# Larger chunks, three homes and waits on the matmuls in a LoRA forward kernel: what 64-row chunks do to a kernel that lives on its DMA queue

## The chip, the cores and the metric

The kernel runs on one core of one Trainium2 chip. The metric is device time in microseconds (us) of one execution; the tables give medians over repeated executions. A verdict of "faster" or "slower" needs a difference of 2% that the whole 95% interval supports; an interval that reaches across 2% is "unclear". With one core a run is called slow when it is over 1.5% above the fastest run of the same kernel; only fast runs are compared here, and one run that stands alone (state unknown) is marked as such.

## The reference

```python
# x: 16 x 2048 x 256 fp32, W: 256 x 256, lora_A: 256 x 16, lora_B: 16 x 256, lora_E: 16
x_flat = x.reshape(-1, in_dim)              # 32768 rows of 256
y = x_flat @ W
lora_out = ((x_flat @ lora_A) * lora_E) @ lora_B
y = y + scale * lora_out
```

The kernel folds the low-rank path into the weight once (W + A·diag(E)·scale·B), so each row of x is read once, multiplied by one 256 x 256 matrix and written once: 33.6 MB in and 33.6 MB out.

## The kernel before

A *chunk* is 32 rows for each of the 128 partitions (4 MB). A *home* is an SBUF tile that holds a chunk; x is loaded into it, and the result is written over x and stored from it. There are eight chunks and six homes, so chunks 6 and 7 reuse the homes of chunks 0 and 1 and must wait for their stores. All large transfers go through one queue, in this order (L is a load, S a store, then chunk, first row, end row):

```python
ROWS = 32; N_CHUNKS = 8; N_HOMES = 6
ORDER = [
    ("L", 0, 0, 8), ("W",), ("L", 0, 8, 16), ("L", 0, 16, 32),
    ("L", 1, 0, 32), ("L", 2, 0, 32), ("L", 3, 0, 32), ("L", 4, 0, 32), ("L", 5, 0, 32),
    ("S", 0, 0, 32), ("S", 1, 0, 24), ("S", 1, 24, 32),
    ("L", 6, 0, 32), ("L", 7, 0, 32),
    ("S", 2, 0, 32), ("S", 3, 0, 32), ("S", 4, 0, 32), ("S", 5, 0, 32), ("S", 6, 0, 32), ("S", 7, 0, 32),
]
HELD = (5, 0)                      # POOL waits here ...
HOLDERS = (("S", 1, 0, 24),)       # ... until this store has landed
```

Compute goes by *groups* of four rows per partition (64 groups): POOL casts x to bf16, PE transposes it, DVE copies the transposed words out of PSUM, PE multiplies, ACT copies the result from PSUM back into the home. PE takes one semaphore for each hand-over with a wait of its own:

```python
def take(s):
    tensor.wait_ge(s, 1).then_inc(s, -1)

def turn(i):
    take(s_stage)
    words = stage[i % NS][:].bitcast(FP32)
    for b in range(CG):
        ins = tensor.transpose(psum_xt[i % NT][:, b, :], words[:, b, :], ident[:])
    ins.then_inc(s_turned, 1)

def multiply(i):
    take(s_xt); take(s_free)
    for b in range(CG):
        for t in range(KT):
            ins = tensor.matmul(psum_y[i % NY][:, b, :], xt[i % NX][:, b, t::KT], weff[:, t, :], ...)
    ins.then_inc(s_y, 1)
# [...] set-up of the folded weight, the other engines' programs, the launch: cut
```

Of the kernel before, what the change touches and what calls it, by code (L numbers as in the profile page):

```python
# [9 lines left out]
BF16 = mybir.dt.bfloat16  # L10
ALU = mybir.AluOpType


ROWS = 32
N_CHUNKS = 8
N_HOMES = 6

ORDER = [
    ("L", 0, 0, 8),
    ("W",),  # L20
    ("L", 0, 8, 16),
    ("L", 0, 16, 32),
    ("L", 1, 0, 32),
    ("L", 2, 0, 32),
    ("L", 3, 0, 32),
    ("L", 4, 0, 32),
    ("L", 5, 0, 32),
    ("S", 0, 0, 32),
    ("S", 1, 0, 24),
    ("S", 1, 24, 32),  # L30
    ("L", 6, 0, 32),
    ("L", 7, 0, 32),
    ("S", 2, 0, 32),
    ("S", 3, 0, 32),
    ("S", 4, 0, 32),
    ("S", 5, 0, 32),
    ("S", 6, 0, 32),
    ("S", 7, 0, 32),
]

HELD = (5, 0)
HOLDERS = (("S", 1, 0, 24),)

WARM_UP = 2

CG = 4
GPC = ROWS // CG
N_GROUPS = N_CHUNKS * GPC

NS, NX, NT, NY = 2, 2, 2, 2  # L50

UNROLL = 4
# [3 lines left out]
def kernel(  # L56
# [16 lines left out]
    KT = K // P  # L73
    assert N == N_CHUNKS * ROWS * P and K == M and KT == 2

    x_chunks = x_flat.rearrange("(c p b) k -> c p b k", p=P, b=ROWS)
    y_chunks = out_flat.rearrange("(c p b) m -> c p b m", p=P, b=ROWS)

    sbuf, psum, sem = nc.alloc_sbuf_tensor, nc.alloc_psum_tensor, tc.alloc_semaphore
    homes = [sbuf(f"home{h}", [P, ROWS, K], FP32) for h in range(N_HOMES)]  # L80
    stage = [sbuf(f"stage{i}", [P, CG, K], BF16) for i in range(NS)]
    xt = [sbuf(f"xt{i}", [P, CG, P * KT], BF16) for i in range(NX)]
    ident = sbuf("ident", [P, P], FP32)

    w_sb = sbuf("w_sb", [P, KT, M], FP32)
# [4 lines left out]
    weff = sbuf("weff", [P, KT, M], BF16)  # L90
    psum_xt = [psum(f"psum_xt{i}", [P, CG, P], FP32) for i in range(NT)]
    psum_y = [psum(f"psum_y{i}", [P, CG, M], FP32) for i in range(NY)]
# [5 lines left out]
        for op in ORDER  # L98
        if op[0] == "S" and (op in HOLDERS or op[1] < N_CHUNKS - N_HOMES)
    }  # L100
    stored = {op: sem(f"stored_{op[1]}_{op[2]}") for op in ORDER if op in waited}
    stored_rest = nc.alloc_semaphore("stored_rest")
    n_rest = sum(op[0] == "S" and op not in waited for op in ORDER)
    ends = sorted((c * ROWS + e) // CG - 1 for kind, c, s, e in (op for op in ORDER if op[0] == "S"))
    s_ident = sem("ident_made")
    s_pe_set_up = sem("pe_set_up")
    s_ate = sem("ate_made")
    s_stage = sem("staged")
    s_turned = sem("turned")
    s_xt = sem("xt_made")  # L110
    s_y = sem("multiplied")
    s_free = sem("y_free")
    s_done = sem("rows_done")

    def home(c):
        return homes[c % N_HOMES]

    sync, gpsimd, scalar, vector, tensor = nc.sync, nc.gpsimd, nc.scalar, nc.vector, nc.tensor
# [20 lines left out]
    def sync_program():  # L139
        for n, op in enumerate(ORDER):  # L140
# [6 lines left out]
            if kind == "L":  # L147
                for st in stored:
                    if st[1] == c - N_HOMES and st[2] < e and s < st[3]:
                        sync.wait_ge(stored[st], 16)  # L150
# [7 lines left out]
    def gpsimd_program():  # L158
        gpsimd.memset(ident[:], 0.0).then_inc(s_ident, 1)  # L159
        gpsimd.wait_ge(s_ident, 1)  # L160
        gpsimd.affine_select(  # L161
            out=ident[:],
            in_=ident[:],
            compare_op=ALU.not_equal,
            fill=1.0,
            base=0,
            pattern=[[-1, P]],
            channel_multiplier=1,
        ).then_inc(s_ident, 1)
        for g in range(N_GROUPS):  # L170
            c, b = g // GPC, g % GPC * CG
            for op, landed in loaded.items():
                if op[1:3] == (c, b):
                    gpsimd.wait_ge(landed, 16)
            if (c, b) == HELD:
                for op in HOLDERS:
                    gpsimd.wait_ge(stored[op], 16)
            if g >= NS:
                gpsimd.wait_ge(s_turned, g - NS + 1)
            gpsimd.tensor_copy(out=stage[g % NS][:], in_=home(c)[:, b:b + CG, :]).then_inc(s_stage, 1)  # L180

        gpsimd.wait_ge(s_turned, N_GROUPS - NS + 1)
        gpsimd.drain().then_inc(s_stage, 1)

    def scalar_program():
        for name, to, of in (
            ("a", a_sb, lora_A.rearrange("(q t) r -> q t r", t=KT)),
            ("e", e_sb, lora_E[:, None]),
            ("b", b_sb, lora_B),
        ):  # L190
            ins = scalar.dma_start(out=to[:], in_=of).then_inc(set_up_loaded[name], 16)
            if name == "a":
                opening.append(ins.ins.name)
        for g in range(N_GROUPS):
            c, b = g // GPC, g % GPC * CG
            scalar.wait_ge(s_y, g + 1)
            scalar.copy(out=home(c)[:, b:b + CG, :], in_=psum_y[g % NY][:]).then_inc(s_free, 1)  # L197
            if g in ends:
                scalar.drain().then_inc(s_done, 1)

    def vector_program():
        vector.wait_ge(set_up_loaded["e"], 16)
        vector.wait_ge(s_pe_set_up, 1)
        vector.tensor_scalar(  # L204
            out=ate[:],
            in0=psum_y[0][:R, :KT, :P],
            scalar1=e_sb[:],
            scalar2=float(scale),
            op0=ALU.mult,
            op1=ALU.mult,  # L210
        ).then_inc(s_ate, 1)
        for g in range(N_GROUPS):
            vector.wait_ge(s_turned, g + 1)
            if g >= NX:
                vector.wait_ge(s_y, g - NX + 1)
            vector.tensor_copy(out=xt[g % NX][:], in_=psum_xt[g % NT][:].bitcast(BF16)).then_inc(s_xt, 1)  # L216
            if g == 0:
                vector.wait_ge(set_up_loaded["w"], 16)
                vector.wait_ge(s_pe_set_up, 2)
                vector.tensor_add(out=weff[:], in0=w_sb[:], in1=psum_y[1][:, :KT, :]).then_inc(s_free, NY)  # L220

    def tensor_program():
        def take(s):
            tensor.wait_ge(s, 1).then_inc(s, -1)  # L224

        def turn(i):
            take(s_stage)

            words = stage[i % NS][:].bitcast(FP32)
            for b in range(CG):  # L230
                ins = tensor.transpose(psum_xt[i % NT][:, b, :], words[:, b, :], ident[:])  # L231
            ins.then_inc(s_turned, 1)

        def multiply(i):
            take(s_xt)
            take(s_free)
            for b in range(CG):
                for t in range(KT):
                    ins = tensor.matmul(  # L239
                        psum_y[i % NY][:, b, :],  # L240
                        xt[i % NX][:, b, t::KT],
                        weff[:, t, :],
                        start=(t == 0),
                        stop=(t == KT - 1),
                    )
            ins.then_inc(s_y, 1)

        tensor.wait_ge(s_ident, 2)
        for i in range(WARM_UP):
            tensor.matmul(psum_y[1][:, :2, :], ident[:], ident[:, None, :].to_broadcast([P, 4, P]), start=True, stop=True)  # L250
        tensor.wait_ge(set_up_loaded["a"], 16)
        for t in range(KT):
            ins = tensor.transpose(psum_y[0][:R, t, :P], a_sb[:, t, :], ident[:])  # L253
        ins.then_inc(s_pe_set_up, 1)
        turn(0)
        tensor.wait_ge(set_up_loaded["b"], 16)
        tensor.wait_ge(s_ate, 1)
        for t in range(KT):
            ins = tensor.matmul(psum_y[1][:, t, :], ate[:, t, :], b_sb[:], start=True, stop=True)  # L259
        ins.then_inc(s_pe_set_up, 1)  # L260
        assert N_GROUPS % UNROLL == 0 and all(UNROLL % n == 0 for n in (NS, NX, NT, NY))
        with tensor.Fori(0, N_GROUPS // UNROLL):
            for i in range(UNROLL):
                turn(i + 1)
                multiply(i)

    def wait_for_stores(nc):
# [4 lines left out]
    with tc.tile_critical(no_gpsimd_drain=True):  # L272
        sync_program()
        gpsimd_program()
        scalar_program()
        vector_program()
        tensor_program()
# [35 lines left out]
```

## Time and profile before

| | before |
|---|---|
| median of the first 3 runs | 161.63 us (161.57 to 162.01) |
| span of the profiled run | 160.4 us |
| bytes moved, mean rate | 67.43 MB, 420 GB/s |
| share of 16 DMA engines on the one large queue | 98.4% |
| busiest compute engine | PE, 60% |

From the profile's page of the kernel before: busy times, then four rows of the slice table (40 equal slices of the span; a digit is a busy share in tenths, PEclk is PE's granted clock), and the large queue's line (packets, MB, share of 16 engines' span).

```profile
PE 96.6 (60%) x782; PEld 84.4 (53%) x782; DVE 45.3 (28%) x66; ACT 66.1 (41%) x65; POOL 67.0 (42%) x70
...
PE   5884958999999999900079999999910000000000
...
POOL 1555417677777787400074777777200000000000
PEclk9999696899999999996556999999996555555555
DMA  7999999999999999999999999999999999999994
...
q1 hardware_dynamic: 2880, 67.37, 98.4%
```

The row to read first is DMA. It is full from the second slice to the last but one, while every compute engine has stopped by slice 30 (118.1 us). This DMA queue, which is never dry, is the limit here (without any compute the time falls by 0.4%, experiment 2), and what stands in it after compute has ended cannot be hurried by compute.

The list of waits of the kernel before, two lines (engine, tile and line, what it waited for: us in total, times, longest):

```profile
POOL stage L180 <- DMA out_dram<-home: 14.0, 1, 14.0
POOL stage L180 <- DMA home<-in_x_dram: 12.0, 4, 4.1
```

The 14.0 us are the hold: POOL stands still at chunk 5 until a store has landed. The issuing queue's timeline of the kernel before (start us, us, engine, line, operation, tiles, count):

```profile
72.75 10.14 SPq L151 DMA_DIRECT2D home<-in_x_dram  x2
82.93 35.58 SPq L156 DMA_DIRECT2D out_dram<-home  x6
```

The last store is issued at 118.2 us, near the end of the second line, but waits its turn in the queue to about 148 us. This is compute's slack. One group of compute at full clock in the timeline of the kernel before (in brackets: idle time before, and its releaser):

```profile
99.77 0.47 PEld L231 LDWEIGHTS psum_xt<-ident,stage 128*128 128x128 f32 x4
99.87 0.60 PE L231 MATMUL psum_xt<-ident,stage 128*128 128x128 f32 x4
...
100.20 0.86 PEld L239 LDWEIGHTS psum_y<-weff,xt 128*128 128x128 bf16 x8
100.31 1.04 PE L239 MATMUL psum_y<-weff,xt 128*128 128x256 bf16 x8
...
101.08 0.47 PEld L231 LDWEIGHTS psum_xt<-ident,stage 128*128 128x128 f32 x4
```

From 99.77 to 101.08 us is one group: 1.31 us, with no gap on PE. The ends overlap the next starts (99.87 + 0.60 us lies behind 100.31), so starts are the safer reading.

### The profile page before, as it was taken

The page shows a single profiled execution, that of the slowest core. Times are in us where ns is not written, and L with a number is a line of the kernel's source. Part 1 is how long each engine was busy: PE and PEld are TensorE (multiplying, and loading weights), DVE is VectorE, ACT ScalarE, POOL GpSimd, SP SyncE. Part 2 cuts the span into 40 slices and gives each one's busy share as a digit, 9 for nine tenths or more (in the row PEclk, how much of TensorE's full clock was granted, in tenths as well). Part 3 has the DMA queues.
Part 4 walks back from the last instruction along what each step waited for, and adds up shares of the span by engine and source line. Part 5 has one row for each costly group of instructions (what it writes and reads, how often), then busy time and mean ns, then how long its engine had stood idle before and what let it go on. Part 6 is the DMA issues. An engine that isn't in the chain of part 4 may idle for free. (4 is left out here: it accounts for less than half of the span.)

```text
span 160.4 us, 2157 instructions
## 1 busy us (share of the span) xinstructions
PE 96.6 (60%) x782; PEld 84.4 (53%) x782; DVE 45.3 (28%) x66; ACT 66.1 (41%) x65; POOL 67.0 (42%) x70
## 2 busy tenths in 40 slices
PE   5884958999999999900079999999910000000000
PEld 2373847899999999900068999999910000000000
DVE  0242332355555555500013555555500000000000
ACT  3034362577777777720004777777730000000000
POOL 1555417677777787400074777777200000000000
PEclk9999696899999999996556999999996555555555
DMA  7999999999999999999999999999999999999994
GB/s 255 395 437 433 482 409 417 474 417 409 458 441 400 449 419 417 409 413 435 394 466 443 449 409 433 427 433 433 441 433 417 441 441 409 458 433 417 449 433 188
DMA packets 3091, 67.43 MB, mean 420 GB/s; under 512 B 512, under 2 KB 528, under 8 KB 656
## 3 DMA queue, kind: packets, MB, share of 16 engines
q1 hardware_dynamic: 2880, 67.37, 98.4%
q10 hardware_dynamic: 208, 0.03, 0.1%
q14 instruction: 3, 0.02, 0.0%
HBM read 33.85 MB, written 33.55 MB: 420 GB/s over the span
## 5 line engine op out<-in xcount | busy, mean ns | idle before, releaser
L197 ACT COPY home<-psum_y 128x1024 f32<-128x1024 f32 x64 | 64.8, 1013 | 50.0 <-PE psum_y L239 50.0
L180 POOL CAST stage<-home 128x1024 bf16<-128x1024 f32 x64 | 66.3, 1042 | 45.2 <-PE psum_xt L231 19.2
L239 PE MATMUL psum_y<-weff,xt 128*128 128x256 bf16 x512 | 70.6, 284 | 0.4 <-PEq L224 0.4
L216 DVE COPY xt<-psum_xt 128x1024 bf16<-128x1024 bf16 x64 | 44.3, 692 | 63.7 <-PE psum_xt L231 63.7
L239 PEld LDWEIGHTS psum_y<-weff,xt 128*128 128x128 bf16 x512 | 52.1, 102 | 7.4 <-issue 0.6
L231 PE MATMUL psum_xt<-ident,stage 128*128 128x128 f32 x260 | 41.5, 285 | 18.0 <-PEq L224 17.8
L231 PEld LDWEIGHTS psum_xt<-ident,stage 128*128 128x128 f32 x260 | 32.1, 148 | 20.5 <-issue 19.6
L250 PE MATMUL psum_y<-ident 128*128 128x512 f32 x4 | 3.6, 1051 | 1.9 <-POOL ident L161 1.9
L250 PEld LDWEIGHTS psum_y<-ident 128*128 128x128 f32 x4 | 1.2, 323 | 3.0 <-POOL ident L161 1.9
L204 DVE TENSOR_SCALAR ate<-psum_y,e_sb 16x256 f32<-16x256 f32 x1 | 0.5, 472 | 5.8 <-DMA e_sb<-in_lora_E_dram 5.8
L197 ACT ACT_TABLE_LOAD x1 | 1.3, 1283 | 2.0 <-issue 2.0
L259 PE MATMUL psum_y<-b_sb,ate 16*128 16x256 f32 x4 | 1.1, 400 | 0.2 <-DMA b_sb<-in_lora_B_dram 0.2
L259 PEld LDWEIGHTS psum_y<-b_sb,ate 16*128 16x128 f32 x4 | 0.7, 184 | 0.5 <-DMA b_sb<-in_lora_B_dram 0.4
L220 DVE TENSOR_TENSOR weff<-w_sb,psum_y 128x512 bf16<-128x512 f32 x1 | 0.7, 689 | 0.7 <-PE psum_y L259 0.7
L253 PEld LDWEIGHTS psum_y<-ident,a_sb 128*16 128x16 f32 x2 | 0.2, 89 | 1.1 <-DMA a_sb<-in_lora_A_dram 1.0
L159 POOL MEMSET ident<- 128x128 f32 x1 | 0.2, 205 | 0.7 <-SPq L272 0.7
L161 POOL TENSOR_SCALAR_AFFINE_SELECT ident<-ident 128x128 f32<-128x128 f32 x1 | 0.3, 294 | 0.2 <-POOL ident L159 0.2
L253 PE MATMUL psum_y<-ident,a_sb 128*16 128x128 f32 x2 | 0.4, 273 | 0.0
L294 POOL MEMSET const-float32-0.0<- 128x1 f32 x1 | 0.1, 99 | 0.2 <-issue 0.2
L294 POOL MEMSET const-bfloat16-1.0<- 128x1 bf16 x1 | 0.1, 102 | 0.0
L294 POOL MEMSET const-uint8-127<- 128x1 uint8 x1 | 0.1, 102 | 0.0
L294 POOL MEMSET const-float32-1.0<- 128x1 f32 x1 | 0.1, 99 | 0.0
## 6 DMA issues: line engine op xcount, KB each, us to landing
home<-in_x_dram SPq DMA_DIRECT2D x7, 4096.0 KB, 30.3
out_dram<-home SPq DMA_DIRECT2D x7, 4096.0 KB, 43.0
out_dram<-home SPq DMA_DIRECT2D x1, 3072.0 KB, 43.1
home<-in_x_dram SPq DMA_DIRECT2D x2, 1024.0 KB, 6.2
home<-in_x_dram SPq DMA_DIRECT2D x1, 2048.0 KB, 11.8
out_dram<-home SPq DMA_DIRECT2D x1, 1024.0 KB, 43.0
w_sb<-in_W_dram SPq DMA_DIRECT2D x1, 256.0 KB, 5.3
a_sb<-in_lora_A_dram ACTq DMA_DIRECT2D x1, 16.0 KB, 5.0
```

What stands on the lines that cost most here:

```text
L161: gpsimd.affine_select(out=ident[:], in_=ident[:], compare_op=ALU.not_equal, fill=1.0, base=0, pattern=[[-1, P]], channel_multiplier=1,).t ...
L180: gpsimd.tensor_copy(out=stage[g % NS][:], in_=home(c)[:, b:b + CG, :]).then_inc(s_stage, 1)
L197: scalar.copy(out=home(c)[:, b:b + CG, :], in_=psum_y[g % NY][:]).then_inc(s_free, 1)
L204: vector.tensor_scalar(out=ate[:], in0=psum_y[0][:R, :KT, :P], scalar1=e_sb[:], scalar2=float(scale), op0=ALU.mult, op1=ALU.mult,).then_in ...
L216: vector.tensor_copy(out=xt[g % NX][:], in_=psum_xt[g % NT][:].bitcast(BF16)).then_inc(s_xt, 1)
L220: vector.tensor_add(out=weff[:], in0=w_sb[:], in1=psum_y[1][:, :KT, :]).then_inc(s_free, NY)
L231: ins = tensor.transpose(psum_xt[i % NT][:, b, :], words[:, b, :], ident[:])
L239: ins = tensor.matmul(psum_y[i % NY][:, b, :], xt[i % NX][:, b, t::KT], weff[:, t, :], start=(t == 0), stop=(t == KT - 1),)
L250: tensor.matmul(psum_y[1][:, :2, :], ident[:], ident[:, None, :].to_broadcast([P, 4, P]), start=True, stop=True)
L253: ins = tensor.transpose(psum_y[0][:R, t, :P], a_sb[:, t, :], ident[:])
L259: ins = tensor.matmul(psum_y[1][:, t, :], ate[:, t, :], b_sb[:], start=True, stop=True)
L294: nc = _bacc.Bacc("TRN2", target_bir_lowering=False, num_devices=1)
```

## The change

The intent: fewer, larger transfers (20 become 16; each partition's part of a store is one run of 64 KB instead of 32 KB); a first chunk that arrives in even pieces; the hold moved to chunk 2, row 16; and PE's hand-overs made cheaper by letting the waits ride on the matmuls, with four semaphores used in turn.

```diff
-ROWS = 32
-N_CHUNKS = 8
-N_HOMES = 6
+ROWS = 64
+N_CHUNKS = 4
+N_HOMES = 3
 ORDER = [
     ("L", 0, 0, 8), ("W",),
-    ("L", 0, 8, 16), ("L", 0, 16, 32), ("L", 1, 0, 32), ... ("L", 5, 0, 32),
-    ("S", 0, 0, 32), ("S", 1, 0, 24), ("S", 1, 24, 32),
-    ("L", 6, 0, 32), ("L", 7, 0, 32),
-    ("S", 2, 0, 32), ... ("S", 7, 0, 32),
+    ("L", 0, 8, 24), ("L", 0, 24, 40), ("L", 0, 40, 64),
+    ("L", 1, 0, 32), ("L", 1, 32, 64), ("L", 2, 0, 16), ("L", 2, 16, 64),
+    ("S", 0, 0, 44), ("S", 0, 44, 64),
+    ("L", 3, 0, 44), ("L", 3, 44, 64),
+    ("S", 1, 0, 64), ("S", 2, 0, 64), ("S", 3, 0, 64),
 ]
-HELD = (5, 0)
-HOLDERS = (("S", 1, 0, 24),)
+HELD = (2, 16)
+HOLDERS = (("S", 0, 0, 44),)
 # [...] s_stage, s_xt and s_free become lists of four semaphores
-        def turn(i):
-            take(s_stage)
+        def turn(i, result=None):
+            staged = s_stage[i % UNROLL]
             for b in range(CG):
+                if b == 0:
+                    tensor.wait_ge(staged, 1)
+                if b == CG - 1 and result is not None:
+                    tensor.wait_ge(s_free[result % UNROLL], 1)
                 ins = tensor.transpose(...)
+                if b == 0:
+                    ins.then_inc(staged, -1)
 # [...] multiply() alike; DVE's wait for s_y, now implied, is gone
```

## The prediction

> **What bounds the kernel now.** The DMA engines. The slice table shows DMA at 9 in every slice but the first and last; the queue table puts 98.4% of 16 engines' span on one queue, which moves 67.37 MB. Packet by packet in the trace, all 16 engines are busy from 1.0 to 158 us, on a plateau of 433 GB/s, with and without compute beside it. [...] 67.37 MB at 433.3 GB/s are 155.5 us of the 160.4 us span. The rest: 1.0 us before the first byte, 2 us of slow first packets, 0.5 us around the small loads (4 to 7 us), 0.45 us where loads turn to stores (58 to 61.5 us), and a tail from 158 us in which the engines finish one by one.
>
> No compute engine is near the path. PE is busy 60%. The chain that ended last stops with ACT's last eviction at 118.1 us; the last store is issued at 118.2 us (DMA queue's timeline), but its packets start around 150 us: some 30 us of slack. POOL's wait for the first stores (14.0 us, list of waits) costs nothing.
>
> **What the change does.**
> - *Bytes*: the same, so the same 155.5 us.
> - *Transfers*: 20 to 16, most packets 64 KB instead of 32 KB. Packets of 16 KB took 611 ns and of 32 KB 1213 ns, so 9 ns each are fixed, about 5 of them not overlapped (estimate). Each engine loses some 56 of 112 large packets: 0.3 us saved, if 64 KB stays one packet; else zero.
> - *First chunk in 8, 16, 16, 24 rows*: a row of all partitions takes 0.30 us at 433 GB/s, so landings at about 4.9, 11.4, 16.2, 23.5 us (estimate). DMA doesn't notice.
> - *Three homes*: chunk 3's first load waits for 44 stored rows of chunk 0. Before, 56 rows had landed at 80.0 us; 12 less are 76.4 us. Behind them 20 rows (6.05 us) still stand in the queue; the fastest engine needs its next packet near 80.5 us; a first byte follows its issue by 1.0 us. Margin about 3 us, no bubble. Later waits have over 10 us.
> - *Hold*: POOL resumes near 76.4 instead of 80.1 us, with 28 groups left instead of 24. At 1.31 us a group, plus the same throttled stretch, compute ends near 118 us; chunk 3's store is needed near 140 us.
> - *PE waits and four semaphores*: PE already runs its 12 matmuls of a group back to back (0.44 + 0.87 = 1.31 us, timeline at full clock). At most hundredths of a us per group, off the path.
>
> **Predicted time: 161.3 us**, 160.4 to 162.3 us in 8 of 10. Chances: faster by over 2% 0.01 (158.4 us is under transfers plus start plus tail), within 2% 0.95, slower by over 2% 0.04.
>
> **What would show it right or wrong.** DMA share 9 in all slices but the ends; plateau 433 to 434 GB/s; no dip at 80 to 82 us (a dip: the 44-row store landed too late) nor at 100 us; packets of 64 KB near 2.42 us; POOL's hold ending near 76 us; PE ending near 118 us; the last store issued over 15 us before its packets move. If the plateau falls, the larger stride or packet costs bandwidth.
>
> **What would make it wrong.** Engines spreading further apart with larger packets, so that some run dry at 80 us or the tail grows; the load-to-store turn at 60 us costing 0 or 1 us instead of 0.45; another address pattern (64 KB between partitions) slowing reads or writes; 64 KB packets handled worse than 32 KB ones.

The forecast's 433.3 GB/s are the trace's (from 125 to 155 us in the kernel before), its 155.5 us are 67.37 MB at that rate, and 161.3 us is the time before (161.63 us) less the 0.3 us for packets. The 5 ns in that gain fit the trace of the kernel before: 2 x 611 - 1213 = 9 ns fixed, less 4 ns, since there a packet of 16 or 32 KB starts 3 to 4 ns (median) before the end of the one ahead of it.

## The result

| | before | after |
|---|---|---|
| median (6 runs each, same rounds) | 161.69 us | 161.72 us |
| lowest, highest | 161.57, 162.37 | 161.33, 162.06 |
| ratio of fast runs | | 0.9993, 95% interval 0.997 to 1.0015 |

A ratio is the mean time of one kernel's fast runs over that of the other's of the same rounds, so it is not quite the ratio of the medians quoted.

The page of the changed kernel, the same rows:

```profile
PE 97.5 (61%) x782; PEld 84.3 (53%) x782; DVE 45.4 (28%) x66; ACT 66.1 (41%) x65; POOL 66.8 (42%) x70
...
PE   5999999959999991000899948999991000000000
...
POOL 1526758477777740001677716777720000000000
PEclk9999999999999999755599995999999555555555
DMA  7999999999999998999999899997997997997991
...
q1 hardware_dynamic: 2304, 67.37, 98.3%
```

The eights and sevens in the DMA row are not gaps: larger packets (2.42 us for 64 KB) fall unevenly into the slices (4.0 us). Counting packets in the trace, 16 are open from 7 us to the tail (of the large queue 15 for about 0.3 us at 80.0, 86.0 and 105.4 us, each time beside a fetch of instructions, which is the sixteenth). POOL's waits and the queue's issues of the changed kernel:

```profile
POOL stage L176 <- DMA out_dram<-home: 17.3, 1, 17.3
...
POOL stage L176 <- DMA home<-in_x_dram: 15.9, 5, 4.2
```

```profile
75.50 7.19 SPq L147 DMA_DIRECT2D home<-in_x_dram  x2
82.73 39.63 SPq L152 DMA_DIRECT2D out_dram<-home  x3
```

The home-reuse load is issued at 75.50 us, when 20 rows of stores still stand in the queue; the last store is issued near 122 us, and its packets start at 138.8 us: 16 to 17 us of slack instead of some 30.

**Reading further than the page: one engine ends last.** Each of the 16 DMA engines gets the same packets and ends each transfer with a packet of 4 bytes (in the changed kernel 16 transfers, 2304 packets: 2048 with data, 8 per transfer and engine, and 256 of 4 bytes, 9 ns each). The times of those 16 marks show how far the engines have drifted apart (from the packet records of each trace; not a view of the page; us from the span's start):

```
end of transfer          before: fastest slowest     after: fastest slowest
loads ahead of 1st store         61.28   62.72              61.23   61.80
stores of homes 0 and 1 (before) / of chunk 0 (after)
                                 80.69   82.12              80.72   81.49
second loads                    100.05  101.88             100.15  101.38
last store                      158.14  159.97             158.11  160.02
```

The fastest engine ends at the same time in both, and so does the slowest, by 0.03 and 0.05 us. At the end of the last store the engines were 1.0 to 3.3 us apart in the traces (without b3_cast_twice_after, whose queue ran dry just before it). In all 14 traces the measured time is the slowest engine's end plus 1.69 to 1.86 us. So two numbers make the time: what an engine needs for its share, and how far the slowest has fallen behind. (The trace gives packets no engine number; one engine is followed from packet to packet, because a new packet starts within some nanoseconds of the end of the one before: for 16 to 64 KB at the median 3 to 4 ns ahead of it.)

### The profile page after: what moved, and what is told of

Read it like the earlier page. It is cut to its first block, busy times and chain, and to the rows that moved or that the text cites. A ratio compares the mean times of both kernels' runs of the same rounds, so it can differ in the third digit from the quotient of the medians.

```text
span 160.5 us, 2023 instructions
## 1 busy us (share of the span) xinstructions
PE 97.5 (61%) x782; PEld 84.3 (53%) x782; DVE 45.4 (28%) x66; ACT 66.1 (41%) x65; POOL 66.8 (42%) x70
## 3 DMA queue, kind: packets, MB, share of 16 engines
q1 hardware_dynamic: 2304, 67.37, 98.3%
## 4 chain that ended last, share of the span: by engine, by line
DMA 55%; PE 17%; POOL 1%; ACT 1%; SPq 1%; issue 1%; ACTq 0%
DMA out_dram<-home 29%; DMA home<-in_x_dram 26%; PE psum_y L237 11%; PE psum_xt L226 6%; POOL stage L176 1%; ACT home L193 1%; SPq L147 1%; SPq L139 0%; ACTq L195 0%; SPq L308 0%; SPq L272 0%
## 5 line engine op out<-in xcount | busy, mean ns | idle before, releaser
L237 PE MATMUL psum_y<-weff,xt 128*128 128x256 bf16 x512 | 69.7, 281 | 0.0
L226 PE MATMUL psum_xt<-ident,stage 128*128 128x128 f32 x260 | 42.1, 286 | 21.2 <-POOL stage L176 21.2
L259 PE MATMUL psum_y<-b_sb,ate 16*128 16x256 f32 x4 | 2.1, 670 | 0.3 <-DMA b_sb<-in_lora_B_dram 0.3
L259 PEld LDWEIGHTS psum_y<-b_sb,ate 16*128 16x128 f32 x4 | 1.2, 319 | 0.9 <-DMA b_sb<-in_lora_B_dram 0.7
```

The costliest lines, as they stand in the source:

```text
L259: ins = tensor.matmul(psum_y[1][:, t, :], ate[:, t, :], b_sb[:], start=True, stop=True)
```

## The experiments

### 1. The two halves of the change, alone

*a1_plan_only* has the new order, homes and hold with the old PE program; *a2_pe_only* has the old order with the new PE program.

> The changed transfers and homes with the old waits on PE. Theory (only the DMA queue counts): 161.7 us, ratio to before 0.998 to 1.002. Rival (two effects cancel: the new PE waits gain, the larger chunks lose): slower than before by 0.5 us or more, ratio 1.003 or over.

> The old transfers and homes with the new waits on PE. Theory: 161.7 us, ratio 0.998 to 1.002, a group of compute at full clock still 1.31 us. Rival (two effects cancel): faster than before by 0.5 us or more, ratio 0.997 or under, and a shorter group.

Measured on one chip, with 11 runs of the kernel before (median 161.82 us): a1 161.63 us, ratio 0.999 (0.9974 to 1.0006); a2 161.80 us, ratio 0.9993 (0.9976 to 1.0011). Both correct. Neither half does anything that these runs resolve. The rival falls.

### 2. DMA alone

All compute is taken out; a store waits only for its rows to have been loaded. Its output is wrong, which doesn't matter for the time.

```diff
-        gpsimd_program(); scalar_program(); vector_program(); tensor_program()
-                sync.wait_ge(s_done, ends.index((c * ROWS + e) // CG - 1) + 1)
+                for ld in loaded:
+                    if ld[1] == c and ld[2] < e and s < ld[3]:
+                        sync.wait_ge(loaded[ld], 16)
```

> Wrong result on purpose: the changed kernel's loads and stores alone, no compute at all; a store waits only for its rows to have landed, so the output is x. Theory (DMA alone sets the time): 161.0 to 161.8 us. Rival (compute beside it slows the transfers or delays them): under 160.5 us, with a higher plateau than 433 GB/s.

161.37 us against 161.84 us before, ratio 0.9959 (0.9927 to 0.9991). The page of this kernel, its DMA rate and DMA row:

```profile
POOL 0.2 (0%) x4
...
DMA  7999999999999998998999899997997997996991
...
q1 hardware_dynamic: 2304, 67.37, 98.4%
```

This is as good as shown a bound can be: without one matmul the time falls by 0.4%. Compute costs something, though, and experiment 5 looks for where. The profiled run was the slowest of the four (161.75 us), and in it the slowest DMA engine ended at 160.06 us, 1.97 us behind the fastest: engines drift that far apart without any compute, too.

### 3. Is the queue's margin real? Store chunk 0 in one piece

```diff
-    ("S", 0, 0, 44),
-    ("S", 0, 44, 64),
+    ("S", 0, 0, 64),
-HOLDERS = (("S", 0, 0, 44),)
+HOLDERS = (("S", 0, 0, 64),)
```

> Chunk 0 is stored by one transfer of 64 rows, so the first load of chunk 3 is issued only when all of it has landed, near 82.4 us, with nothing left in the queue. Theory (the split at row 44 is what keeps the queue full, with a margin of about 3 us): the 16 engines run dry for about 2 us, 163.5 to 164.3 us, ratio 1.011 to 1.017, and a hole in the DMA row near 82 us. Rival (a gap there is made up later or hidden): 161.7 us.

165.37 us, ratio 1.0212 (1.0186 to 1.0238): slower beyond noise, by 3.5 us instead of the expected 2, although the verdict is "unclear", since the interval reaches below 2%. Slices of the DMA row of this kernel:

```profile
DMA  7999999999999997996598989899989989969992
GB/s 256 367 435 447 431 427 463 423 447 431 391 511 395 443 511 335 495 479 303 255 351 353 452 377 419 350 513 495 399 383 495 431 351 511 479 287 511 479 415 128
```

The hole is in slices 19 and 20 (6 and 5, 303 and 255 GB/s). By the packet records the fastest engine had nothing from 80.5 us to about 83.4 us, of which 1.6 us passed until the slowest engine had ended as well (82.05 us). Fifteen of the first 16 packets after the hole took 0.4 to 1.0 us longer than the 1.67 us that is usual for 44 rows (the first packets of the whole run are slow, too: 8 KB took up to 1.09 us in the kernel before and 1.17 us in the changed one, with a median of 0.31 us), and the next turn from loads to stores, at 101 to 104 us, was dearer by 1.0 us on the fastest engine. The direction was right and the size was not: here the dry queue cost its gap and then a second start. The split at row 44 is what avoids this.

### 4. What a packet costs: 4 KB packets in the same 16 transfers

Rows are dealt to partitions in groups of four, so a run of memory is 4 KB. (The order of addresses changes with it.)

```diff
-    x_chunks = x_flat.rearrange("(c p b) k -> c p b k", p=P, b=ROWS)
+    x_chunks = x_flat.rearrange("(c b p g) k -> c p b (g k)", p=P, b=ROWS // CG, g=CG)
 # the same for y_chunks; the home is viewed as 16 runs of CG * K
```

> The changed kernel with the same 16 transfers, but rows dealt to partitions in groups of four, so that every packet is 4 KB (1024 data packets per engine instead of 120). Theory of the prediction (9 ns per packet, about 5 ns of them not overlapped): 904 x 5 ns = 4.5 us more, 165 to 167 us. Rival 1 (nothing of it is overlapped): 8 us more, near 169.8 us. Rival 2 ([...]the packet size costs nothing at 4 KB and over, so the 0.3 us of the prediction was no gain at all): 161.7 us.

166.51 us, ratio 1.029 (1.0255 to 1.0325), correct. The fastest engine ended at 163.74 us instead of 158.11: 5.63 us for 904 more packets, 6.2 ns each. The estimate of about 5 ns nearly held. What makes up the cost of a packet is not shown here.

The same number shows what the change could have saved. An engine had 160 data packets before (20 transfers of 8) and has 128 after. 32 packets of 6.2 ns are 0.2 us. In the steady stores at the end it is there: two 32-row stores took the fastest engine 19.37 us before (138.77 to 158.14), one 64-row store takes 19.32 us (138.79 to 158.11).

### 5. The hold: does POOL's wait cost nothing?

*a3_no_hold* is the changed kernel and *c3_before_no_hold* the kernel before, each without the hold. No race arises: what POOL then reads has its own wait for its load.

```diff
-            if (c, b) == HELD:
-                for op in HOLDERS:
-                    gpsimd.wait_ge(stored[op], 16)
```

> The changed kernel without POOL's wait at chunk 2 row 16. Theory: the hold is off the path: 161.7 us, ratio 0.998 to 1.002; compute ends some 12 to 18 us earlier (before 110 us instead of near 121 us), the DMA plateau stays at 433 to 434 GB/s. Rival (the hold keeps compute away from the turn of loads to stores, and that is worth time): 0.5 us or more slower, with a deeper dip of the DMA rate at 60 us.

> The kernel before without POOL's wait at chunk 5. Theory (one DMA engine loses about 6% while compute runs beside stores, and the hold keeps compute away from the first stores): slower by 0.4 to 1.0 us, ratio 1.003 to 1.006, and in the trace one slow packet every 1.3 us between 66 and 80 us. Rival (the loss without the hold is peculiar to the changed kernel's chunks): ratio 0.998 to 1.002.

a3: 162.54 us, ratio 1.0046 (1.003 to 1.0061). c3: 162.42 us against 161.77 us, ratio 1.0038 (1.0013 to 1.0062). Taking away an idle wait of 14 to 17 us leaves either kernel some 0.7 us slower than the kernel before (the changed kernel with its hold stands at 0.9993). For a3 that was the rival's time and a miss of the theory; but the rival's mechanism, compute at the turn near 60 us, is not it: POOL stood idle there (from 58.3 us with the hold, from 58.6 to 63.3 us without), and the loss at that turn, 0.25 us per engine in the changed kernel and 0.52 us in a3, is 0.75 us in the run without any compute. It varies from run to run for a reason that no run here shows. The theory of c3 was formed after a3's trace; its time and its slow packets came as expected, but its trace does not join the two (below). What a3 expected of the end of compute was wrong too: its last store was issued near 124 us, no earlier than with the hold, because POOL then ran into the next thing that was missing. POOL in the timelines, first the changed kernel, then a3:

```profile
57.23 1.04 POOL L176 CAST stage<-home 128x1024 bf16<-128x1024 f32 x1 [0.27 <-PE psum_xt L226]
75.59 2.02 POOL L176 CAST stage<-home 128x1024 bf16<-128x1024 f32 x2 [17.32 <-DMA out_dram<-home]
```

```profile
63.26 3.01 POOL L173 CAST stage<-home 128x1024 bf16<-128x1024 f32 x3 [4.66 <-DMA home<-in_x_dram]
...
78.60 1.04 POOL L173 CAST stage<-home 128x1024 bf16<-128x1024 f32 x1 [0.27 <-PE psum_xt L223]
96.34 2.02 POOL L173 CAST stage<-home 128x1024 bf16<-128x1024 f32 x2 [16.70 <-DMA home<-in_x_dram]
```

With the hold, compute is idle from 60 to 75 us, while the queue stores chunk 0. Without it, POOL works from 63 to 80 us (ACT to 83 us), beside those stores, and then idles from 80 to 96 us, while the queue loads. The idle time has only moved, but to the wrong side, as the packets show. Packets after 62 us that took over 38 ns longer than the median of their size (start in us : ns too long; from the packet records, turns near 80 and 100 us left out):

```
after                86.3:662
                     103.2:155 105.7:246 105.8:155 108.3:160 110.9:146 113.5:155 116.0:146 118.6:150 121.2:144 123.7:51
before                63.9:99  65.2:85   66.5:61   67.7:52   84.8:214
                     103.1:75  104.4:80  105.7:80  107.0:80  108.3:85  109.6:89  110.9:89  112.2:85
                     113.5:71  114.8:71  116.1:52  118.5:127 119.9:61
c3, before, no hold   63.7:80  65.0:85   66.3:80   67.5:80   68.8:80   70.1:94 [...] 77.2:60  78.2:42, and from 103.6 to 121.7 much as before
DMA alone            none between 62 and 80, one from 102 on
```

The list of the changed kernel has from 103.2 us on, but for one entry, a spacing of 2.57 us, which is one 64 KB packet (2418 ns) plus 150 ns: one engine, one packet after the other, each 6% too long. (In the kernel before: 1.30 us, a 32 KB packet of 1213 ns plus 80 ns.) The list starts when compute meets stores and ends within 2 us of the end of compute (122.0 and 118.1 us; in the kernel before the last two entries start after it); between 84 and 98 us, where compute runs beside loads, neither kernel has such a train; and without compute there is none. So, in these traces, compute that runs beside stores slows one of the 16 engines by about 6%. In the changed kernel the eight entries from 103.2 to 121.2 us that follow one another add up to 1.2 us. The odd entries, 86.3:662 and 105.7:246 (84.8:214 in the kernel before), each stand beside a fetch of instructions (8 KB, at 86.0, 105.4 and 84.5 us).

**Does the slowed engine set the time?** Only where it ends last, and that differs from trace to trace. The end marks of the last store (us behind the fastest engine):

```
                       slowed engine   last of the others
changed kernel              1.91            1.23
a3, no hold                 2.47            1.83
before                      1.75            1.83
c3, before, no hold         2.38            2.49
DMA alone                   none            1.97
```

In the changed kernel and in a3 it set the time, by about 0.7 and 0.6 us. In the kernel before and in c3 another engine ended last, one that had fallen behind at the start and at the turns; between 103 and 158 us the distance from fastest to slowest did not grow at all. So the one trace of c3 does not show that the slow packets made it slower. What both traces without the hold show is that the slowed engine falls some 0.6 us further behind (2.4 to 2.5 us against 1.8 to 1.9). That this is the measured 0.7 us, over runs in which the other engines end at random, is an inference. With the 4 KB packets of experiment 4 the effect is there too: from 104.6 to 124.7 us some 100 packets, spaced like those of one engine, add up to about 0.9 us; but it fell on an engine that was early, and the engines were no further apart at the end (1.0 us). The hold does what its place suggests: it keeps compute out of the first stores.

### 6. Is it the bytes or the instructions?

One look at DMA alone, with the last six stores of 32 rows each and one engine working beside each: POOL's casts, ACT's copies, DVE's copies, PE's groups, then DVE copies of one element. One run. Its output is wrong, which doesn't matter for the time.

```diff
+        gpsimd.wait_ge(loaded[("L", 3, 44, 64)], 16)        # then 9 casts
+        scalar.wait_ge(stored[("S", 1, 0, 32)], 16)         # then 8 copies psum_y -> a stored part of a home
+        vector.wait_ge(stored[("S", 1, 32, 64)], 16)        # then 10 copies psum_xt -> xt
+        tensor.wait_ge(stored[("S", 2, 0, 32)], 16)         # then 6 groups of 12 matmuls
+        vector.wait_ge(stored[("S", 2, 32, 64)], 16)        # then 64 copies of one element
```

> Wrong result on purpose: the loads and stores alone, the last three chunks stored in halves of 32 rows (six stores of 9.7 us, packets of 32 KB, 1213 ns each). Beside each of the first five, one engine works alone: first POOL casts, then ACT copies, DVE copies, PE's groups of 12 matmuls, then 64 one-element DVE copies; beside the sixth nothing. In the traces so far one of the 16 DMA engines is slower by about 80 ns in each 32 KB packet while all of compute runs beside stores. Theory A (the data that POOL, ACT or DVE move to or from SBUF get in its way): 20 ns or more per packet in the first three windows, none in the fourth and fifth. Theory B (it is something per instruction, not per byte): most of it in PE's window (24 instructions in 1.3 us) and in the window of tiny copies, under 15 ns in the first three. If no window shows it, it needs the engines together, and that stays open.

The timeline of this kernel gives the windows:

```profile
101.78 9.86 POOL L176 CAST stage<-home 128x1024 bf16<-128x1024 f32 x9 [100.06 <-DMA home<-in_x_dram]
...
112.81 8.31 ACT L184 COPY home<-psum_y 128x1024 f32<-128x1024 f32 x8
121.21 7.22 DVE L199 COPY xt<-psum_xt 128x1024 bf16<-128x1024 bf16 x10 [115.69 <-DMA out_dram<-home]
...
140.44 11.17 DVE L204 COPY ate<-e_sb 1x1 f32<-1x1 f32 x64 [12.02 <-DMA out_dram<-home]
```

PE worked from 130.9 to 141.5 us, at half speed up to 135.8 us (a group took 2.6 us instead of 1.31, although the granted clock in the trace is 1.00 there). Packets over 12 ns too long (same form as above):

```
POOL, ACT, DVE windows (101.8 to 128.5)   101.8:14  110.2:23  120.0:20
PE window, half speed                     130.9:28  132.1:14  133.4:23  134.6:23
PE window, full speed                     135.8:52  137.1:52  138.3:61  139.6:88  140.9:52
one-element copies                        142.2:23  143.4:14  144.6:19  145.9:23  147.1:23  148.3:33  149.3:376  149.6:32  150.8:42  152.1:127
```

The big copies of POOL, ACT and DVE leave the packets alone (three of them 14 to 23 ns too long). PE's groups lengthen them by 52 to 61 ns (once 88) of the 80 that all of compute costs, at half speed by 14 to 28 ns, and DVE copies of four bytes, which move next to nothing, lengthen them by 14 to 42 ns. (Of the two odd entries, 149.3:376 stands beside a fetch of instructions at 149.0 us, and 152.1:127 starts after the last copy has ended.) In this one run it goes with the number of instructions, not with the bytes: theory B. What on the chip does it is open, and since every timed run here comes with a recorded span and clock, whether an untraced run has the effect is open as well.

### 7. How much slack is left: POOL casts every group twice

```diff
-            gpsimd.tensor_copy(out=stage[g % NS][:], in_=...).then_inc(s_stage..., 1)
+            gpsimd.tensor_copy(out=stage[g % NS][:], in_=...).then_inc(s_twice, 1)
+            gpsimd.wait_ge(s_twice, g + 1)
+            gpsimd.tensor_copy(out=stage[g % NS][:], in_=...).then_inc(s_stage..., 1)
```

> The changed kernel with POOL casting each group twice (second cast behind the first): a group takes about 2.2 us or more instead of 1.31 us, so compute ends near 150 us, after the 139.6 us at which the packets of the last store (64 rows) are due. Theory (slack near 18 us, then the delay comes through in full): 168 to 174 us, with the DMA row empty from 140 us to the last store's issue.

> The kernel before with POOL casting each group twice. Compute ends near 150 us as in the changed kernel, but its last store is 32 rows and due only near 150 us. Theory: 161.5 to 164 us, so the change has given up some 10 us of slack that its time doesn't show. Rival (slack doesn't depend on the size of the last store): as slow as the changed kernel with the cast doubled.

With a group of 2.1 us, the changed kernel took 167.54 us, ratio 1.0344 (1.0311 to 1.0378), just under the expected range; the kernel before 162.86 us, ratio 1.0052 (1.0019 to 1.0085), within it. The page of the changed kernel with the double cast:

```profile
POOL 1849999999999999999999999999999999000000
...
DMA  7999999899999989999999899979989991099595
```

and that of the kernel before with it:

```profile
POOL 1798969999999999999999999999999999800000
...
DMA  7999999999999999999999999999999999999990
```

Compute ends near 145 us in both (150 was expected: a group was to take 2.2 us). The changed kernel's queue runs dry from about 140 to 146 us (the 1 and 0), because its last store is 64 rows and due at 139 us; the kernel before has a last store of 32 rows, due at 148 us. What the change gave up is slack that its time doesn't show. The kernel before lost 1.0 us even so, though its queue never ran dry: in its trace the slow packets of experiment 5 go on to 146.7 us, and its slowest engine ended at 161.28 us with the fastest at 157.95. That slowest engine is the slowed one: the next was only 1.46 us behind the fastest. Of all traces this one shows most plainly that the effect can set the time.

### 8. Where the 0.2 us of the packets went

Every trace of the new transfers with large packets (a1, a3, b1, b3, c4, d1 and the changed kernel, seven in all) has packets that are too long between 79 and 82.5 us, at the turn from stores to loads: 0.18 to 0.29 us per engine. The traces of the old transfers (before, a2, b4, c3) and of 4 KB packets have 0.01 us or less there. Ahead of that turn stands a store of 8 rows in the old order (8 KB packets) and of 20 rows in the new one (20 KB). *e1_small_last_store* changes only that:

```diff
-    ("S", 0, 44, 64),
+    ("S", 0, 44, 56),
+    ("S", 0, 56, 64),
```

> The changed kernel with chunk 0 stored in 44, 12 and 8 rows instead of 44 and 20, so that the packets just ahead of the turn from stores to loads at 80 us are 8 KB as in the kernel before (and not 20 KB). In the traces so far every run of the changed transfers with large packets lost 0.18 to 0.29 us per engine between 79 and 82.5 us, and no run of the old transfers or of 4 KB packets lost over 0.01 us. Theory (the size of the last store packets makes that dip): it falls under 0.05 us and the time is 0.1 to 0.3 us lower than the changed kernel's, ratio to before 0.996 to 0.999, hardly resolved by the timing. Rival (the loads behind it, of 44 rows, make the dip): it stays at 0.18 us or more.

The loss at the turn fell to 0.02 us. The time was 161.75 us against 161.90 us before, ratio 0.999 (0.9966 to 1.0014). So the dip goes with the last store in these traces, and with the size of its packets rather than its rows: the run with 4 KB packets also stores 20 rows there, and has no dip. The gain in time is below what five rounds resolve.

### 9. A version meant to beat both

If compute beside stores costs about 85 ns a group (an estimate, near the upper end of the 71 to 89 ns of the kernel before from 103.1 to 114.8 us, one entry in 1.30 us, about one a group), three groups more before the hold should give 0.25 us.

```diff
-    ("L", 2, 16, 64),
+    ("L", 2, 16, 32),
+    ("L", 2, 32, 64),
-HELD = (2, 16)
+HELD = (2, 28)
```

> The changed kernel with chunk 2's second load split at row 32 and the hold at row 28: three more groups are computed while loads still run, three fewer beside stores. Theory (about 85 ns lost per group beside stores on the slowest engine): 0.25 us faster than the changed kernel, ratio to before 0.996 to 0.999. Rival: no difference, ratio 0.999 to 1.001. The difference is near what five rounds can resolve.

162.13 us against 161.77 us, ratio 1.0006 (0.9982 to 1.003): no gain. But the edit did not do what it was meant to. In its trace the loads ahead of the first store end at 61.3 to 62.7 us, while the three added groups run until 66.5 us (ACT's last copy): they run largely beside the first stores, where packets are too long again (63.2:89, 64.9:47). And they were not taken from the later stores: POOL only waits longer for chunk 3 (7.46 us instead of 4.16), whose 16 groups start at 96.2 us and end at 122.7, as in the changed kernel (95.8 and 122.0). So this run does not test the theory. Besides, its engines were 1.3 us apart by the fourth transfer (15.19 to 16.52 us; changed kernel 14.79 to 15.57 us), and this spread of the start, which differs from run to run, is larger than the gain that was sought. No version is shown to beat either kernel.

## Why the prediction was right

The time, 161.72 us, lies in the stated range and the class "within 2%" came true. The bound was understood; that the number came so near proves less, since "no change" (161.69 us) would have come nearer, and the gain of 0.3 us in the prediction did not show in the time. Point by point:

- **The bound.** Right, and shown by DMA alone (0.4% less) and by the two halves alone (0.1% or less).
- **433 GB/s "with and without compute beside it".** Right to about half a per cent (by the packet records 431.7 GB/s from 103 to 118 us and 433.3 from 125 to 155 us before; 431.8 and 434.2 after), and wrong in the place that matters. The plateau hides that one engine of 16 loses about 6% while compute runs beside stores. The prediction saw the tail "in which the engines finish one by one" and gave no cause; this is part of it in the changed kernel's trace (0.7 of 1.91 us), but not in that of the kernel before.
- **Packets.** A 64 KB packet took 2418 ns, as said (2.42 us), and the fixed part of 5 ns not overlapped came out at 6.2 ns. The number of packets saved was wrong: 32 per engine and not 56, since only stores became 64 rows long and most loads stayed shorter. So 0.2 us instead of 0.3 us, and the turn at 80 us cost as much again (0.2 to 0.3 us).
- **"No dip at 80 to 82 us (a dip: the 44-row store landed too late)."** The step that failed. There was a dip, and it did not mean that: the store landed at 75.5 us, 0.9 us earlier than predicted, all engines had packets, and the packets themselves were slow. Experiment 8 traces it to the size of the last store's packets.
- **The margin.** Real. Without the split the queue ran dry and 3.5 us were lost.
- **The hold.** It ended at 75.59 us (predicted near 76). That POOL's wait "costs nothing" is true but too weak: the wait is worth some 0.7 us.
- **Landings of the first chunk.** 4.8, 11.1, 16.0 and 23.3 us, predicted 4.9, 11.4, 16.2 and 23.5. DMA did not notice them.
- **End of compute.** 122.0 us instead of 118. The term left out is POOL's wait of 4.16 us, at 91.6 us, for chunk 3's first 44 rows, which come as one transfer. The last store still was issued over 16 us before its packets moved (over 15 predicted).
- **PE waits.** A group stayed at 1.31 us, and a2 alone had ratio 0.9993.

## What to carry to other kernels

When one DMA queue is full from end to end, as here (98.3 and 98.4% of 16 engines' span), look for what fewer transfers and cheaper hand-overs can buy: here 6.2 ns per packet and nothing that the runs resolve. Count the packets that really go away, and check that a queue behind a reuse of buffers keeps work (the changed kernel issued the reusing load at 75.5 us, about 5 us before the fastest engine came to the end of its stores at 80.7 us), because the dry queue of experiment 3 cost more than its gap (3.5 us for 2.9 us). Then look below the mean rate: the transfers here ended with the slowest of 16 engines (the last store 1.0 to 3.3 us after the fastest), so plot the engines' ends, not only the plateau, and check that the engine that is slowed is also the one that ends last before you put time down to it. And don't remove an idle wait because its engine is off the critical path (here it was worth some 0.7 us) before you know which transfers it keeps apart from which work.
